# Attention: splits of the Fourier branch's projection weights ordered behind the turned probabilities three steps ahead of their use

## The chip, the core and the metric

The kernel runs on one core of one Trainium2 chip. The metric is the device time of one execution in microseconds (us), the median over runs; lower is better. Engines are named as in the profile: PE (TensorE, matmul), PEld (its weight loads), DVE (VectorE), ACT (ScalarE), POOL (GpSimd) and SP (SyncE, which issues DMAs here).

## The reference, cut to what matters

One block of a diffusion backbone, in fp32: 512 latent tokens, 256 context tokens, width 2048. Attention has 12 query heads and 4 key heads of 128; a Fourier branch of width 512 runs beside it. Both are gated, projected to width 2048 and merged.

```python
def block(qi):
    s = jnp.einsum('bqhgd,bkhd->bhgqk', qi, k, preferred_element_type=jnp.float32)
    w = jax.nn.softmax(s, axis=-1).astype(v.dtype)
    return jnp.einsum('bhgqk,bkhd->bqhgd', w, v)
...
y_a = (attn * jax.nn.silu(z_a)) @ w_pa
y_b = (_fourier_mix(u_b) * jax.nn.silu(z_b)) @ w_pb
return (g_a * y_a + g_b * y_b) @ w_o
```

The product that this case turns on is the one with `w_pb`, whose rows lie behind those of `w_pa` in one tensor, `w_pab`.

## The kernel before

**Numbers as pairs.** A fp32 operand is split into a high part (ACT, L181: a copy rounded to fp32r) and a low part (DVE, L182: the source less the high part). A product is then three matmuls (`mm3`, L339 to L341: high by high, low by high, high by low, in the order of the lines). Every weight that comes from memory is split so: it lands in a raw buffer (`wr`, L217, issued by SP; some land in one of four tiles `R`), and `split_piece` makes `whi` and `wlo` of it, 128x1024 each. The raw buffer is free for the next load once `wlo` is made.

**The attention stage.** It has 48 steps, one for each head and block of 128 queries, with a loop over `i` in the program. In a step, `scores(i)` makes 128x768 scores on PE, DVE finds their maximum (L1533), ACT takes the exponential into `probs` (L1535). `turn(i - 1)` transposes the probabilities of the step before in six 128x128 pieces on PE (L1551) into one region of PSUM, and splits them from there: ACT writes `pth` (L181, 128x768), DVE `ptl` (L182). Two turns fill one pair `pth`, `ptl` of 256 queries, and `values` multiplies a pair with the values (18 matmuls of 256 columns). The region into which probabilities are turned is one (`wide[3]`), so the next turn's transposes wait until `ptl` of the turn before has read it. Three more regions (`wide[0]` to `wide[2]`) take scores in rotation, and now and then the transposed keys of the next key head (`get_keys`, L1389). `wide[2]` and `wide[3]` share a PSUM bank.

**The filler.** Between these, `fill` puts pieces of the Fourier branch's projection on PE: for each of four chunks of 512 output columns and each of four blocks of tokens, 12 matmuls with the weights `whi`, `wlo` of two pieces of `w_pab` (in the trace: `banks<-whi,s` 128x512), into one bank; DVE multiplies it with the gate (L1499) and so frees the bank for the next block. The two pieces of the first chunk are made ahead of the attention stage. The six others bear these names in the order of the instructions: `whi_6810` and `whi_6830` (second chunk, raw `wr_6455` and `wr_6457`), `whi_7335` and `whi_7355` (third, `wr_6915` and `wr_6917`), `whi_7850` and `whi_7870` (fourth, `wr_7436` and `wr_7438`). Each `wlo` has the next number.

**Other work of the stage.** DVE also sums gate weights (L1369, 128x1024, from raw buffers), scales attention by its gate (L1577, L1587) and makes forms of the next stage's operand (L1618 to L1624). ACT scales gates by the softmax's sums (L1545) and copies turned gates out of PSUM (L1576, after the transposes L1566). `turn_queries` (L1396) turns and splits queries. POOL loads heads and gates and adds up weights for the next stage by DMA.

**What sets the order.** In the attention stage no order is written out for any engine: a scheduler places each engine's instructions by dependencies and by its own estimates of durations, working through the program in order. Once placed, ACT, DVE, POOL and SP run their queues strictly in that order, and so does PE with its matmuls. `tc.issue_after(x)` around an instruction keeps the scheduler from placing that instruction ahead of `x`; it names an order and no data. `get` (L298) splits the piece that is asked for and up to three pieces behind it in the stream (`look`), so in program order a piece of `w_pab` is split long ahead of its use. Before the change nothing held such a split back (`in_line` is empty until the last stage), and the scheduler placed it wherever ACT and DVE had room by its estimate.

Of the kernel before, what the change touches and what calls it, by code (L numbers as in the profile page):

```python
# [27 lines left out]
NKEY = T + C  # L28
KT = NKEY // P
# [44 lines left out]
def context_piece(g, name, pc):  # L74

    n = 28 * (g - NQZ) + 4 * ONE_GROUP.index(name) + pc
    if n % 2 == 0 and 0 <= n < 8:
        return "cn", n // 2
    if n % 7 == 4 and 18 <= n < 46:
        return "cr", n // 7 - 2  # L80
# [43 lines left out]
def block_kernel(ctx, tc, xT, ctx_rows, ctx_toks, x, c_row, w_ss, w_gate, vecs, qkg, rope, dft_c, dft_s,  # L124
# [32 lines left out]
    def uid(s):  # L157
        cnt[0] += 1
        return f"{s}{cnt[0]}"
# [20 lines left out]
    def split_from(src, hi, lo):  # L180
        first = nc.scalar.activation(hi, src, ACT.Copy)  # L181
        return first, nc.vector.tensor_tensor(lo, src, hi.bitcast(F32), op=ALU.subtract)  # L182
# [61 lines left out]
    def hl_tiles():  # L244
        if more_hl and not more_hl[0]:
            hl_pools.extend(range(MORE_HL))
            more_hl.clear()
        elif more_hl:
            more_hl[0] -= 1
        hl_pools.append(hl_pools.pop(0))  # L250
        pool = hl_pools[-1]
        if isinstance(pool, tuple):
            return [slot_tile(p, (1024,), F32R) for p in pool]
        if isinstance(pool, int):
            return int_tiles(pool)
        return [pool.tile([P, 1024], F32R, tag=t, bufs=hl_pools.count(pool), name=uid("w" + t)) for t in ("hi", "lo")]


    last_split, split_of, in_line, context_sub, chained = [], [], [], [], []

    look = [1]

    def split_piece(e):
        if e.out is not None or e.kind == "raw":
            return
        raws = [r for _, r in e.raws]
        src = raws.pop(0) if e.stage is None else chain[e.pc]
        for r in raws:
            nc.vector.tensor_tensor(src, src, r, op=ALU.add)
        if e.off:  # L270
            with ExitStack() as line:
                if e.key == ("P7", KV, 3):
                    line.enter_context(tc.issue_after(context_sub[-1].ins))
                if e.key[1] in DIFF_IN_LINE:

                    line.enter_context(tc.issue_after(split_of[-2][1].ins))
                nc.vector.tensor_tensor(src, chain[e.pc], src, op=ALU.subtract)
        hi, lo = e.dst() if e.dst else hl_tiles()
        if isinstance(hi, Halves):
            for k in range(2):  # L280
                last_split.append(split_from(src[:, 512 * k : 512 * k + 512].rearrange("p (a c) -> p a c", a=2),
                                             hi.parts[k], lo.parts[k]))
        else:
            hi, lo = hi[:, : e.cols], lo[:, : e.cols]
            with ExitStack() as line:
                if in_line:
                    for i in last_split[-1]:
                        line.enter_context(tc.issue_after(i.ins))
                last_split.append(split_from(src, hi, lo))
        split_of.append(last_split[-1])  # L290
        if e.nxt is not None:
            chained[:] = [nc.gpsimd.dma_start(chain[e.pc], e.nxt, accum_op=ALU.add)]  # L292
        if e.stage == 3:
            left[e.pc] = 0
        r = lambda t: t if isinstance(t, Halves) else t.rearrange("p (n m) -> p n m", n=e.n)
        e.out = (r(hi), r(lo))

    def get(key):  # L298
        load_more()
        turn = [e for e in ahead if not e.aside]  # L300
        assert turn[0].key == key, (turn[0].key, key)
        for e in turn[: min(look[0], len(hl_pools))]:
            if e is turn[0] or e.key[0] != "V":
                split_piece(e)
        load_more()
        e = turn[0]
        ahead.remove(e)
        free.extend(p[0::2] for p, _ in e.raws if p in retired)
        return e.raws[0][1] if e.kind == "raw" else e.out
# [17 lines left out]
    def take(shape, dt=F32, pool=None):  # L327
        p = next((p for p in free if p[0] is pool), free[0])
        free.remove(p)
        t = slot_tile(p, shape, dt)  # L330
        home[id(t)] = p, t
        return t

    def give(*ts):
        free.extend(home.pop(id(t))[0] for t in ts)
# [86 lines left out]
    for g in range(LAST + 1):  # L422
        for name in ONE_GROUP:
# [6 lines left out]
            for pc in range(4):  # L430
                p = context_piece(g, name, pc)
# [4 lines left out]
            for pc in range(4):  # L436
                if (g, name, pc) in GATE_AT:
                    q = GATE_AT[g, name, pc]
                    stream(("gate", q), w_gate[q], 1024, 1, "raw")
                    e = todo.pop()  # L440
# [4 lines left out]
    q = NGATE  # L445
# [300 lines left out]
    def split_next():  # L746
        e = next(e for e in ahead if e.out is None and e.kind != "raw")
        split_piece(e)
        e.raws = []
# [27 lines left out]
    with tc.manual_schedule(engines={E.PE}):  # L777
# [6 lines left out]
        with tc.manual_schedule(engines={E.Activation, E.DVE}):  # L784
# [25 lines left out]
            for kb in range(1, 4):  # L810
                k = kb + 1
# [32 lines left out]
            for kb in range(4, KK - 4, 2):  # L844
# [6 lines left out]
                k = kb + 2  # L851
# [100 lines left out]
    for g in range(4):  # L952
        gate_b(g)
        positions(g)
        if g < 2:
            tokens(g + 2)
        with behind((finals[-1], low[g if g < 2 else 3])):
            for e in ahead[:g]:
                split_piece(e)
            for z, y in products[2 * g - 4 : 2 * g - 2] if g > 1 else ():  # L960
                nc.vector.tensor_tensor(z, y, z, op=ALU.mult)
# [554 lines left out]
    probs, pts, AT, A1, A2 = {}, {}, {}, {}, {}  # L1516
# [30 lines left out]
    def turn(i):  # L1547
        p = probs.pop(i)
        tp = wide[3]
        for k in range(KT):  # L1550
            nc.tensor.transpose(tp[:, k * P : (k + 1) * P], p[:, k * P : (k + 1) * P], ident)  # L1551
        if i % 2 == 0:
            pts[i // 2] = [atp.tile([P, KT, 256], F32R, tag=n, bufs=2, name=uid(n)) for n in ("pth", "ptl")]
        c = slice((i % 2) * P, (i % 2) * P + P)
        split_from(tp[:, :NKEY].rearrange("p (k q) -> p k q", k=KT), *(w[:, :, c] for w in pts[i // 2]))
        give(p)

    def values(half):
# [127 lines left out]
    for i in range(NSTEP + 3):  # L1686
# [13 lines left out]
        if 1 <= i <= NSTEP:  # L1700
            turn(i - 1)
            divide(i - 1)
# [14 lines left out]
        if i == 3:  # L1717
            with tc.issue_after(maxima[0].ins), tc.issue_after(maxima[1].ins):
                e = take((1024,))
# [350 lines left out]
```

## Time and profile before

| what | value |
|---|---|
| median of 3 runs | 1287.12 us (1286.21 to 1287.29) |
| the profiled execution | 1286.97 us |
| its span in the profile | 1285.2 us |
| attention stage in the trace | about 803.6 to 1009 us of the span |
| granted TensorE clock, mean | 0.999 |

The profiled execution took 1286.97 us, 1.8 us more than its span. In timelines a row is start in us, duration in us, engine, line, operation, output and inputs (buffer numbers left out), shape and count; in square brackets stands how long the engine was idle before it and what ended that. Matmuls are pipelined, and the shown duration of one reaches into the next, so PE's real pace is read from the starts. An engine's row with "q" is its instruction queue.

### The profile page before, as it was taken

Reading aid. Unit: us, or ns where it says so; the run is one execution under the profiler, and the core shown is the slowest. Engines: PE = TensorE matmul, PEld = TensorE weight load, DVE = VectorE, ACT = ScalarE, POOL = GpSimd, SP = SyncE. Lnnn points to the kernel's source line nnn. Section 1 sums busy time; section 2 is a strip of 40 time slices with the busy share of each in tenths; the row PEclk is TensorE's granted clock in tenths of the full one; section 3 lists DMA queues with packets and bytes.
Section 4 is the critical chain, followed back from the end, with each engine's and each line's share of the span. In section 5 each row is a group of like instructions: output and inputs, shape, how many; then the busy total and the mean of one; then the engine's idle time right before and its main releaser. Section 6 shows DMA issues by size and latency. Waiting matters only on the chain.

```text
span 1285.2 us, 17638 instructions
## 1 busy us (share of the span) xinstructions
PE 1269.6 (99%) x6562; PEld 1045.2 (81%) x6562; DVE 991.0 (77%) x1305; ACT 683.2 (53%) x1077; POOL 173.2 (13%) x226
## 2 busy tenths in 40 slices
PE   8999999999999999999999999999999999999997
PEld 5677888888888888888888888888888888888886
DVE  5767899889778787748687756778898777787677
ACT  5322765555466564543355445766667646465544
POOL 0000121111102011012021011011100221211310
PEclk9999999999999999999999999999999999999999
DMA  9998798888898998887879897578852989998986
GB/s 378 412 368 344 242 204 254 229 240 239 234 315 209 320 271 254 291 197 188 282 204 288 254 259 234 180 234 250 265 178 67 260 241 258 245 207 222 227 207 179
DMA packets 104343, 319.07 MB, mean 248 GB/s; under 512 B 9889, under 2 KB 32801, under 8 KB 100289
## 3 DMA queue, kind: packets, MB, share of 16 engines
q1 hardware_dynamic: 54336, 195.24, 41.8%
q0 software_dynamic: 27600, 100.29, 37.0%
q10 hardware_dynamic: 22320, 22.42, 5.1%
q8 instruction: 51, 0.84, 0.3%
q14 instruction: 36, 0.29, 0.1%
HBM read 283.30 MB, written 34.61 MB: 247 GB/s over the span
## 4 chain that ended last, share of the span: by engine, by line
PE 82%; DVE 3%; DMA 2%; ACT 2%; issue 1%; SPq 0%; ACTq 0%
PE banks L339 10%; PE banks L340 10%; PE banks L341 10%; PE x L341 9%; PE x L339 9%; PE x L340 9%; PE y L341 8%; PE y L340 8%; PE y L339 8%; PE banks L1551 2%; DMA wr<-in_w_pab 1%; DVE wlo L182 1%; DMA s<-yb_d 1%; PE banks L1665 1%; DVE s L182 0%
## 5 line engine op out<-in xcount | busy, mean ns | idle before, releaser
L181 ACT ACTIVATE whi<-R 128x1024 fp32r<-128x1024 f32 x138 | 145.1, 1058 | 143.7 <-PE banks L341 47.5
L182 DVE TENSOR_TENSOR wlo<-R,whi 128x1024 fp32r<-128x1024 f32 x138 | 167.7, 1221 | 61.2 <-ACT whi L181 60.9
L182 DVE TENSOR_TENSOR wlo<-wr,whi 128x1024 fp32r<-128x1024 f32 (+1 forms) x122 | 147.3, 1213 | 62.7 <-ACT whi L181 62.5
L181 ACT ACTIVATE whi<-wr 128x1024 fp32r<-128x1024 f32 (+1 forms) x122 | 127.4, 1050 | 123.4 <-PE y L341 33.0
L339 PE MATMUL banks<-whi,s 128*128 128x512 f32 (+1 forms) x400 | 157.8, 394 | 0.9 <-ACT ev L1160 0.7
L340 PE MATMUL banks<-wlo,s 128*128 128x512 f32 (+1 forms) x400 | 155.9, 390 | 0.0
L341 PE MATMUL banks<-whi,s 128*128 128x512 f32 (+1 forms) x400 | 155.8, 389 | 0.0
L339 PE MATMUL x<-whi,s 128*128 128x512 f32 x352 | 137.1, 390 | 0.0
L341 PE MATMUL x<-whi,s 128*128 128x512 f32 x352 | 137.0, 389 | 0.0
L340 PE MATMUL x<-wlo,s 128*128 128x512 f32 x352 | 136.9, 389 | 0.0
L292 POOL DMA_DIRECT2D R<-in_w_g x68 | 59.5, 874 | 484.7 <-DVE wlo L182 290.2
L340 PE MATMUL y<-wlo,s 128*128 128x512 f32 x316 | 123.0, 389 | 0.1
L339 PE MATMUL y<-whi,s 128*128 128x512 f32 x316 | 122.9, 389 | 0.0
L341 PE MATMUL y<-whi,s 128*128 128x512 f32 x316 | 122.8, 389 | 0.0
L181 ACT ACTIVATE s<-wr 128x512 fp32r<-128x512 f32 (+2 forms) x93 | 60.8, 677 | 66.0 <-DMA wr<-cf_d 24.4
L182 DVE TENSOR_TENSOR s<-wr,s 128x512 fp32r<-128x512 f32 (+2 forms) x93 | 66.7, 749 | 31.8 <-ACT s L181 30.9
L339 PEld LDWEIGHTS banks<-whi,s 128*128 128x128 f32 x400 | 75.2, 188 | 16.6 <-ACT ev L1160 1.1
L341 PEld LDWEIGHTS banks<-whi,s 128*128 128x128 f32 x400 | 75.2, 188 | 15.3
L340 PEld LDWEIGHTS banks<-wlo,s 128*128 128x128 f32 x400 | 75.2, 188 | 13.9 <-DVE wlo L182 0.2
L340 PEld LDWEIGHTS x<-wlo,s 128*128 128x128 f32 x352 | 66.1, 188 | 13.8
L341 PEld LDWEIGHTS x<-whi,s 128*128 128x128 f32 x352 | 66.1, 188 | 13.7
L339 PEld LDWEIGHTS x<-whi,s 128*128 128x128 f32 x352 | 66.1, 188 | 13.6
(333 smaller groups left out, 2794.0 us busy)
## 6 DMA issues: line engine op xcount, KB each, us to landing
wr<-in_w_g SPq DMA_DIRECT2D x124, 512.0 KB, 5.6
R<-in_w_g POOLq DMA_DIRECT2D x68, 512.0 KB, 7.4
wa<-in_w_ss SPq DMA_DIRECT2D x31, 1024.0 KB, 9.5
R<-in_w_g SPq DMA_DIRECT2D x32, 512.0 KB, 5.8
wr<-in_w_gate SPq DMA_DIRECT2D x32, 512.0 KB, 5.1
wr<-in_w_o SPq DMA_DIRECT2D x24, 512.0 KB, 7.1
R<-in_w_o POOLq DMA_DIRECT2D x24, 512.0 KB, 8.9
wr<-in_w_pab SPq DMA_DIRECT2D x20, 512.0 KB, 6.1
```

What stands on the lines that cost most here:

```text
L181: first = nc.scalar.activation(hi, src, ACT.Copy)
L182: return first, nc.vector.tensor_tensor(lo, src, hi.bitcast(F32), op=ALU.subtract)
L292: chained[:] = [nc.gpsimd.dma_start(chain[e.pc], e.nxt, accum_op=ALU.add)]
L339: nc.tensor.matmul(o, ah, bh, start=start, stop=False, skip_group_check=cont)
L340: nc.tensor.matmul(o, ah, bl, start=False, stop=False, skip_group_check=cont)
L341: nc.tensor.matmul(o, al, bh, start=False, stop=stop, skip_group_check=cont)
L1551: nc.tensor.transpose(tp[:, k * P : (k + 1) * P], p[:, k * P : (k + 1) * P], ident)
L1665: last_turn[0] = nc.tensor.transpose(tp[:, k // 2, 256 * (k % 2) + P * t : 256 * (k % 2) + P * t + P], m[:, t, k * P : k * P + P], ident)
```

## The change

`turn` appends the two instructions of its split (`pth` on ACT, `ptl` on DVE) to a list `turned_low`. When `split_piece` splits a piece of `w_pab` for the filler (key `pab`), both of its instructions may be placed only behind the third-last pair of that list, that is, behind the split of the probabilities that were turned three turns back in program order. For the two pieces of the first chunk the list is still empty, and nothing changes. In the last stage (`in_line`) the old rule stays. No instruction is added or taken away.

```diff
-    last_split, split_of, in_line, context_sub, chained = [], [], [], [], []
+    last_split, split_of, in_line, context_sub, chained, turned_low = [], [], [], [], [], []
...
-                if in_line:
-                    for i in last_split[-1]:
-                        line.enter_context(tc.issue_after(i.ins))
+                for i in last_split[-1] if in_line else turned_low[-6:-4] if e.key[0] == "pab" else ():
+                    line.enter_context(tc.issue_after(i.ins))
                 last_split.append(split_from(src, hi, lo))
...
-        split_from(tp[:, :NKEY].rearrange("p (k q) -> p k q", k=KT), *(w[:, :, c] for w in pts[i // 2]))
+        turned_low.extend(split_from(tp[:, :NKEY].rearrange("p (k q) -> p k q", k=KT), *(w[:, :, c] for w in pts[i // 2])))
```

What the scheduler makes of it shows in the order of the instructions. The file is one line shorter from L286 on, so the rows of after bear line numbers lower by one for the same code (L1551 reads L1550 there). Up to the attention stage and after it the order is the same on every engine, except where named below.

The first place is ACT's queue where the second chunk's pieces are soon due (`pth_6718` is written twice, for two turns). Before:

```order
L181 ACTIVATE pth_6718<-banks 128x6x128
L181 ACTIVATE s_6604<-s_6601 128x256
L1545 ACTIVATE s_6263<-s_6263,gain 128x128
L1535 ACTIVATE s_6784,gain<-banks,gain 128x768
L181 ACTIVATE s_6805<-banks 128x512
L1545 ACTIVATE s_6513<-s_6513,gain 128x128
L181 ACTIVATE pth_6718<-banks 128x6x128
L181 ACTIVATE whi_7335<-wr_6915 128x1024
L1535 ACTIVATE s_6841,gain<-banks,gain 128x768
L181 ACTIVATE pth_6795<-banks 128x6x128
```

And after:

```order
L181 ACTIVATE pth_6718<-banks 128x6x128
L1575 COPY R_1342<-banks 128x256
L1544 ACTIVATE s_6513<-s_6513,gain 128x128
L181 ACTIVATE whi_6810<-wr_6455 128x1024
L181 ACTIVATE whi_6830<-wr_6457 128x1024
L181 ACTIVATE s_6604<-s_6601 128x256
L181 ACTIVATE pth_6718<-banks 128x6x128
L1534 ACTIVATE s_6784,gain<-banks,gain 128x768
L181 ACTIVATE s_6805<-banks 128x512
L181 ACTIVATE pth_6795<-banks 128x6x128
```

`whi_7335` has left the place ahead of `pth_6795` (it stands 40 rows later now, behind the first `pth_7240`), and `whi_6810` and `whi_6830` have come in ahead of the second `pth_6718`. Before, `whi_6810` stood ahead of the attention stage and `whi_6830` four rows ahead of the first `pth_6718`.

The second place is PE's queue at the same steps, between the turns of `s_6706` and `s_6735`. Before, these rows stood between the six transposes of the one and the six of the other:

```order
L341 MATMUL banks<-s_6335,s_6645 128x512
L339 MATMUL banks<-s_6335,s_6645 128x256
L340 MATMUL banks<-s_6336,s_6645 128x256
L341 MATMUL banks<-s_6335,s_6645 128x256
L339 MATMUL banks<-whi_6450,s_6409 128x512
L340 MATMUL banks<-wlo_6451,s_6409 128x512
L341 MATMUL banks<-whi_6450,s_6410 128x512
L339 MATMUL banks<-pth_6718,s_6341 128x256
L339 MATMUL banks<-s_6335,s_6645 128x512
L340 MATMUL banks<-s_6336,s_6645 128x512
L341 MATMUL banks<-s_6335,s_6645 128x512
L1551 MATMUL banks<-ident,s_6735 128x128 x6
```

And after, behind the transposes of `s_6706` and one matmul of the filler:

```order
L1395 MATMUL banks<-ident,s_6648 128x128 x4
L1388 MATMUL banks<-ident,wr_6442 128x128 x4
L338 MATMUL banks<-s_6335,s_6645 128x512
L339 MATMUL banks<-s_6336,s_6645 128x512
L340 MATMUL banks<-s_6335,s_6645 128x512
L338 MATMUL banks<-whi_6450,s_6409 128x512
L339 MATMUL banks<-wlo_6451,s_6409 128x512
L340 MATMUL banks<-whi_6450,s_6410 128x512
L338 MATMUL banks<-s_6335,s_6645 128x256
L339 MATMUL banks<-s_6336,s_6645 128x256
L340 MATMUL banks<-s_6335,s_6645 128x256
L1550 MATMUL banks<-ident,s_6735 128x128 x6
```

More of PE's work lies between the two turns now. The last two of the six transposes of keys (L1389, `wr_6442`) stand behind `s_6735`'s turn in both. Between the turn and these two came 17 matmuls of 256 columns before; now there are 3 of 512 columns and 8 of 256.

The third place is DVE's queue some twenty steps later, where the fourth chunk's first piece has come to. Before:

```order
L182 TENSOR_TENSOR ptl_7758<-banks,pth_7757 128x6x128
L1533 TENSOR_REDUCE gain<-banks 128x1
L1577 SCALAR_TENSOR_TENSOR s_7633<-banks,R_1342 128x256
L1533 TENSOR_REDUCE gain<-banks 128x1
L1544 RECIPROCAL gain<-gain 128x1
L1369 SCALAR_TENSOR_TENSOR wr_7573,gparts<-wr_7573,crow_5349 128x1024
L182 TENSOR_TENSOR ptl_7758<-banks,pth_7757 128x6x128
L182 TENSOR_TENSOR s_7867<-wr_7419,s_7866 128x768
L182 TENSOR_TENSOR s_7841<-banks,s_7841 128x512
```

And after:

```order
L182 TENSOR_TENSOR ptl_7758<-banks,pth_7757 128x6x128
L182 TENSOR_TENSOR wlo_7851<-wr_7436,whi_7850 128x1024
L1532 TENSOR_REDUCE gain<-banks 128x1
L1576 SCALAR_TENSOR_TENSOR s_7633<-banks,R_1342 128x256
L1532 TENSOR_REDUCE gain<-banks 128x1
L1543 RECIPROCAL gain<-gain 128x1
L1368 SCALAR_TENSOR_TENSOR wr_7573,gparts<-wr_7573,crow_5349 128x1024
L182 TENSOR_TENSOR s_7841<-banks,s_7841 128x512
L182 TENSOR_TENSOR ptl_7758<-banks,pth_7757 128x6x128
L182 TENSOR_TENSOR s_7867<-wr_7419,s_7866 128x768
L182 TENSOR_TENSOR wlo_7871<-wr_7438,whi_7870 128x1024
```

`wlo_7851` has come in behind the first `ptl_7758`. Before, it stood 41 rows earlier, between the two `ptl_7317`, with `whi_7850` between the two `pth_7316` on ACT.

`whi_7355` and `whi_7870` keep their places within two or three rows. On SP, the loads of the stage stand in another order (`wr_6915` behind two gate pieces and the values `wr_6894`, and a gate piece `wr_7763` five loads later), since raw buffers come free in another order. On POOL, three issues have changed places with a neighbour, and the store of the gate sums (L1746) stands five issues later.

## Prediction

> **What bounds the kernel now.** I read first the busy times of the page, then the windows of 10 us through the attention stage, and in the windows that stand out the timeline of each engine.
>
> ```profile
> PE 1269.6 (99%) x6562; PEld 1045.2 (81%) x6562; DVE 991.0 (77%) x1305; ACT 683.2 (53%) x1077; POOL 173.2 (13%) x226
> ```
>
> PE is the bound: only time in which PE waits can be won, and all that can be lost is new waiting of PE. The change touches the order of the attention stage alone (about 803.6 to 1009 us of the span of 1285.2), so I looked for PE's waits there. Windows, with busy time and instructions of PE, PEld, DVE, ACT and POOL, then the granted clock, the DMA share and GB/s:
>
> ```profile
> 830.00:840.00 10.00, 10.00 (x70) 8.89 (x69) 9.11 (x17) 7.77 (x17) 0.55 (x1) 1.00 0.84 219
> 840.00:850.00 10.00, 8.78 (x58) 7.22 (x57) 7.66 (x12) 5.97 (x10) 2.13 (x4) 1.00 0.64 217
> 890.00:900.00 10.00, 9.71 (x61) 8.12 (x60) 9.40 (x15) 6.09 (x12) 1.60 (x3) 1.00 0.74 208
> 940.00:950.00 10.00, 9.64 (x66) 8.53 (x65) 9.57 (x16) 7.22 (x14) 1.49 (x3) 1.00 0.68 209
> ```
>
> The first is a window without a wait; the three others hold PE's waits near a chunk's first weights (places A, B and C). The clock was full in all of them. PE's rows there:
>
> ```profile
> 841.26 0.39 PE L340 MATMUL banks<-s,s 128*128 128x512 f32 x1
> 841.50 0.40 PE L341 MATMUL banks<-s,s 128*128 128x512 f32 x1
> 842.30 0.87 PE L1551 MATMUL banks<-ident,s 128*128 128x128 f32 x6 [0.40 <-DVE ptl L182]
> ...
> 844.77 0.28 PE L340 MATMUL banks<-ptl,s 128*128 128x256 f32 x1
> 844.89 0.28 PE L341 MATMUL banks<-pth,s 128*128 128x256 f32 x1
> 845.99 0.44 PE L1389 MATMUL banks<-ident,wr 128*128 128x128 f32 x2 [0.82 <-DVE ptl L182]
> ...
> 891.91 0.39 PE L341 MATMUL banks<-whi,s 128*128 128x512 f32 x1
> 892.38 0.39 PE L339 MATMUL banks<-pth,s 128*128 128x256 f32 x1
> ...
> 897.26 0.39 PE L341 MATMUL banks<-s,s 128*128 128x512 f32 x1
> 897.87 0.50 PE L339 MATMUL banks<-whi,s 128*128 128x512 f32 x1 [0.22 <-DVE R L1499]
> ...
> 947.99 0.28 PE L339 MATMUL banks<-pth,s 128*128 128x256 f32 x1
> 948.62 0.39 PE L339 MATMUL banks<-s,s 128*128 128x256 f32 x1 [0.36 <-ACT s L1535]
> ```
>
> Starts tell PE's pace: a matmul of 512 columns takes 0.24 (841.26 to 841.50), one of 256 takes 0.12 (844.77 to 844.89). What is over in a step from start to start is waiting: A1, 841.50 to 842.30, 0.80 - 0.24 = 0.56; A2, 844.89 to 845.99, 1.10 - 0.12 = 0.98; B1, 891.91 to 892.38, 0.47 - 0.24 = 0.23; B2, 897.26 to 897.87, 0.61 - 0.24 = 0.37; C, 947.99 to 948.62, 0.63 - 0.12 = 0.51. Together 2.65 us, 0.2% of the time. Behind each stands a split of the filler's weights, on ACT, on DVE, or on both.
>
> **The change part by part.**
>
> Nothing is added or removed; seven of the twelve instructions for six pieces move far. One moved piece takes 0.97 us of ACT's queue (842.30 to 843.27, below) and 1.23 of DVE's.
>
> *Place A, `whi_7335` goes.* ACT's and DVE's rows:
>
> ```profile
> 836.28 0.81 ACT L181 ACTIVATE pth<-banks 128x768 fp32r<-128x768 f32 x1
> ...
> 839.83 0.81 ACT L181 ACTIVATE pth<-banks 128x768 fp32r<-128x768 f32 x1
> 842.30 1.07 ACT L181 ACTIVATE whi<-wr 128x1024 fp32r<-128x1024 f32 x1 [1.66 <-DMA wr<-in_w_pab]
> 843.27 0.88 ACT L1535 ACTIVATE s<-banks,gain 128x768 f32<-128x768 f32 x1
> ...
> 844.14 0.80 ACT L181 ACTIVATE pth<-banks 128x768 fp32r<-128x768 f32 x1
> ```
> ```profile
> 837.92 0.95 DVE L182 TENSOR_TENSOR ptl<-banks,pth 128x768 fp32r<-128x768 f32 x1
> ...
> 841.29 0.95 DVE L182 TENSOR_TENSOR ptl<-banks,pth 128x768 fp32r<-128x768 f32 x1
> ...
> 843.40 1.23 DVE L182 TENSOR_TENSOR wlo<-wr,whi 128x1024 fp32r<-128x1024 f32 x1 [0.56 <-ACT whi L181]
> 844.98 0.96 DVE L182 TENSOR_TENSOR ptl<-banks,pth 128x768 fp32r<-128x768 f32 x1 [0.35 <-ACT pth L181]
> ```
>
> ACT stood 1.66 us at `whi_7335`, whose weights had not landed. Behind it in ACT's queue stood an exponential and `pth_6795`, then on DVE `ptl_6796`, and PE's last two key transposes (L1389) waited for that: this is A2. With the split gone from here, `pth` can begin when the transposes end (842.30 + 0.87 = 843.17), 0.97 us earlier than 844.14. From their end to the next allowed transposes is 844.14 to 844.98 on ACT and 844.98 to 845.99 on DVE, 0.84 + 1.01 = 1.85 us. But PE's own order changed as well: between turn and the two L1389 stand 3 matmuls of 512 and 8 of 256 columns now, 3 x 0.24 + 8 x 0.12 = 1.68 us, counted from the start behind the transposes. Six transposes took 842.30 to 844.89 less 16 x 0.12, that is 0.67 (0.11 each), so that start lies 0.20 ahead of their modelled end. 1.85 + 0.20 - 1.68 = 0.37; with a little for ACT's start I say that 0.40 of A2's 0.98 stays and 0.58 goes.
>
> The wait is there although the two L1389 write other columns than `ptl` reads: `wide[2]` and `wide[3]` share a bank. The Trainium skill, PSUM — Partial Sum Buffer, section on bank collisions, says to guard PSUM by bank and quadrant and not by address. By that rule the 0.40 stays, and the trace agrees (0.82 us idle at 845.99, ended by `ptl`); guarded by address, it would go and the sum below would be 0.40 larger.
>
> *Place A, `whi_6810` and `whi_6830` come in.* They stand ahead of the second `pth_6718` (839.83), and the turn at 842.30 waits for that one's `ptl` (841.29): A1. From the first `pth_6718` (836.28) to the second took 3.55 us. In the new queue stand there the first itself (0.81), 2 x 0.97 of the two pieces, and a copy, a scaling and `s_6604` of at most 256 columns (0.3 each, a third of the 0.81 for 768): 3.65, 0.10 more. On DVE, from one `ptl` to the next took 3.37 (837.92 to 841.29); `wlo_6811` (1.23) has come in, while `s_6805` (512 columns, two thirds of 0.95) and idle time have left: a few tenths more at most. So I expect the second `ptl` up to 0.2 later, 0.6 if ACT's copy must wait for its transposes. PE meanwhile has more to do between the turns: 7 x 0.24 + 8 transposes of 0.11 + 3 x 0.12 = 2.92, where 7 x 0.24 + 4 x 0.12 = 2.16 stood, 0.76 more. A wait of 0.56 with 0.76 of work before it and 0.2 of delay behind it is gone; with 0.6 of delay, 0.40 of it stays. I take it as gone, 0.56. Where these two pieces stood, nothing on PE waits for them.
>
> *Place B, `whi_7850` goes and `whi_7335` comes in.*
>
> ```profile
> 884.97 0.90 ACT L1535 ACTIVATE s<-banks,gain 128x768 f32<-128x768 f32 x1 [0.58 <-DVE gain L1533]
> ...
> 895.38 1.06 ACT L181 ACTIVATE whi<-wr 128x1024 fp32r<-128x1024 f32 x1 [1.23 <-DMA wr<-in_w_pab]
> ```
> ```profile
> 887.28 0.42 DVE L1577 SCALAR_TENSOR_TENSOR s<-banks,R 128x256 f32<-128x256 f32 x1 [1.12 <-ACT R L1576]
> ...
> 888.38 0.96 DVE L182 TENSOR_TENSOR ptl<-banks,pth 128x768 fp32r<-128x768 f32 x1 [0.67 <-ACT pth L181]
> ...
> 889.63 1.23 DVE L182 TENSOR_TENSOR wlo<-wr,whi 128x1024 fp32r<-128x1024 f32 x1
> ...
> 891.64 0.68 DVE L182 TENSOR_TENSOR s<-banks,s 128x512 fp32r<-128x512 f32 x1
> ...
> 896.73 0.42 DVE L1577 SCALAR_TENSOR_TENSOR s<-banks,R 128x256 f32<-128x256 f32 x1 [0.59 <-ACT R L1576]
> 897.14 0.67 DVE L1499 TENSOR_TENSOR R<-banks,R 128x512 f32<-128x512 f32 x1
> ```
>
> B2: ACT stood 1.23 us for the weights of `whi_7850`; behind it the copy of turned gates (L1576), DVE's L1577 and L1499 ran late, and L1499 frees the bank that the filler waited for (897.87). The piece is gone from here, and 0.37 with it. B1: PE waits for the split at 891.64, which stands behind `wlo_7356` (889.63). In the new order `wlo_7356` stands behind that split and a gate: 0.23 goes. `whi_7335` comes in just ahead of the exponential at 884.97, where ACT has 0.58 of idle time; `wlo_7336` comes where DVE has 1.12 + 0.67 of it, more than its 1.23. I cost it at nothing; without that cover it costs up to 1.23. Its DMA will have landed (see the loads below).
>
> *Place C, `whi_7850` comes in at about 933 us.*
>
> ```profile
> 947.59 0.90 ACT L1535 ACTIVATE s<-banks,gain 128x768 f32<-128x768 f32 x1
> ```
> ```profile
> 934.77 0.96 DVE L1533 TENSOR_REDUCE gain<-banks 128x1 f32<-128x768 f32 x1 [0.71 <-PE banks L341]
> ...
> 936.59 0.96 DVE L1533 TENSOR_REDUCE gain<-banks 128x1 f32<-128x768 f32 x1 [0.54 <-PE banks L341]
> ```
>
> `wlo_7851` adds 1.23 on DVE; DVE's idle time ahead of the next two reductions is 0.71 + 0.54 = 1.25. It fits with 0.02 to spare, so I expect no cost, but this is the weakest cover. The wait at 948.62 is for the exponential at 947.59. In the new order 5 of the filler's matmuls (5 x 0.24 = 1.2) stand ahead of the scores that wait, more than the 0.51; of it I take 0.40, leaving something for the narrow cover.
>
> *Loads.* SP's loads of the stage and three of POOL's issues change order, since raw buffers are held longer. The loads of this kind land 6.1 us after issue:
>
> ```profile
> wr<-in_w_pab SPq DMA_DIRECT2D x20, 512.0 KB, 6.1
> ```
>
> Followed through the raw buffers, each is issued over 15 us ahead of its use in either order (an estimate from the places of the issues); no cost, and one late load would cost up to 6.1.
>
> *The sum:* 0.58 + 0.56 + 0.37 + 0.23 + 0.40 = 2.14 us. Does it pass through? Behind the stage PE hardly waits for anything that time would not bring along:
>
> ```profile
> PE banks L1665 <- DMA s<-yb_d: 0.7, 1, 0.7
> ```
>
> This is PE's one wait after 1009 us that a DMA ends, and its 0.7 us may stay. So the profiled 1286.97 us (1.8 above its span, 0.15 below the median) would become 1284.8, and the median 1287.12 becomes 1284.98.
>
> **The rivals.**
>
> *1. More goes than the five waits.* Weight loads stop as well when PE is held back by less than a whole matmul. PEld falls from 8.89 in the quiet window to 7.22, 8.12 and 8.53: 1.67 + 0.77 + 0.36 = 2.80, and at 0.889 a us that is 3.15 us of PE's time near the three places. If all goes, 1287.12 - 3.15 = 1284.0. For it: ACT's queue loses both long DMA waits (1.66 and 1.23). Against it: A2's 0.40 should stay. Perfetto Trace Analysis in the Trainium skill (Identifying the Most-Contended Engine) has it that matmul busy time is a poor measure for TensorE and weight-load busy time a good one. By matmul busy time the three windows miss only 1.22 + 0.29 + 0.36 = 1.87 us, which would give 1285.25; the five waits by starts are 2.65, so the trace agrees that busy time shows too little.
>
> *2. Given back at C.* If DVE's gaps at 934 no longer come where they did, one piece's 1.23 ends on PE's path and C's 0.40 isn't won: 1284.98 + 0.40 + 1.23 = 1286.6. For it: 0.02 of margin.
>
> *3. Slower.* DVE is the second engine, 9.40 and 9.57 of 10 us at B and C. If `whi_7850`, `wlo_7851` and then `whi_7870`, `wlo_7871` end last on the chain from scores to turned probabilities, each piece costs 1.06 on ACT and 1.23 on DVE in a row: 2 x 2.29 = 4.58, and C's 0.40 is lost: 1284.98 + 4.98 = 1290.0. It decides once PE's reductions at 934 to 937 leave less than the 1.23 us that move in. Against it: filler work on PE covers a late turn for about 1 us each.
>
> *4. The waits are replaced by others.* The scheduler's order rests on its estimates of durations; the same pieces go through the same engines, and PE may wait as long elsewhere: 1287.1.
>
> **How the numbers follow.** My forecast, the sum, has a chance of 0.42 and a range of its own of 1284.3 to 1285.7 (A2's 0.40 also gone and 0.3 elsewhere; A1's 0.40 and 0.3 of C staying). Rival 1 has 0.24, rival 2 0.14, rival 3 0.10, rival 4 0.10. About 0.2% of 1287, 2.6 us, is what a measurement of this kernel can tell from no change: below 1284.55 is faster, above 1289.7 slower. A third of the forecast's own range, 0.14, lies below, and rival 1: 0.38 faster. The rest of the forecast, 0.28, and rivals 2 and 4 make 0.52 same. Rival 3 makes 0.10 slower. The range goes from rival 1 with another 0.6 (the quiet window itself may hold small waits) to rival 4 with 0.3: 1283.4 to 1287.4; rival 3 lies outside.
>
> **What would show each step.** In the profile after: ACT's idle time ended by DMA of `in_w_pab` in the stage should fall from 1.66 + 1.23 to nearly nothing (A2, B2). The turn that stood at 842.30 should follow its predecessor without a wait, and the two key transposes wait some 0.4. At 933 DVE should run `wlo_7851` without a later row on PE waiting for a reduction, an exponential or a turn. PEld near the three places should come to about 8.5 of 10 us each. The prediction is wrong if PE waits over 0.5 us anywhere that it didn't (first at C, then ahead of 884.97), or if a load ends ACT's idle time at a new place.

## The result, and the profile after

| kernel | median of runs, us | lowest to highest | runs |
|---|---|---|---|
| before | 1286.71 | 1286.21 to 1287.29 | 6 |
| after | 1293.62 | 1292.93 to 1294.03 | 6 |

The ratio is 1.0053, with a 95% interval of 1.004 to 1.0066: 6.9 us slower, where 2.1 us faster was forecast. The profiled execution of after took 1293.67 us, its span is 1291.9 (1285.2 before). The first line of the page says that PE did the same matmuls with 1.9 us more of busy time, and so stood idle about 5 us longer:

```profile
PE 1271.5 (98%) x6562; PEld 1047.7 (81%) x6562; DVE 990.7 (77%) x1305; ACT 682.0 (53%) x1077; POOL 174.4 (13%) x226
```

**In this pair of profiles the attention stage won about what was forecast.** The four windows of the prediction, now in after (columns as there):

```profile
830.00:840.00 10.00, 10.00 (x69) 9.07 (x68) 8.73 (x16) 8.10 (x15) 0.55 (x1) 1.00 0.74 208
840.00:850.00 10.00, 9.95 (x65) 8.26 (x64) 9.52 (x16) 5.93 (x13) 2.75 (x5) 1.00 0.80 269
890.00:900.00 10.00, 10.00 (x70) 9.09 (x69) 9.35 (x14) 5.81 (x12) 2.42 (x4) 1.00 0.80 270
940.00:950.00 10.00, 10.00 (x71) 8.99 (x70) 9.40 (x15) 7.25 (x14) 1.59 (x4) 1.00 0.69 261
```

PE is busy all through at B and C, and for all but 0.05 us at A. The view of PE's waits in the stage keeps one line, at its start; before there were five:

```profile
PE banks L338 <- ACT ev L1159: 0.7, 1, 0.7
```

PE came to the stage 0.18 us earlier than before (its first matmul of the filler starts at 803.42, before at 803.60) and left it 2.00 us earlier. The loss lies behind the stage. These are the last matmul ahead of the first transposes of a merged chunk (L1665 before, L1664 after), the transposes, and one matmul some way on, in before and then in after:

```profile
1033.37 0.40 PE L341 MATMUL banks<-whi,s 128*128 128x512 f32 x1
1033.61 1.04 PE L1665 MATMUL banks<-ident,s 128*128 128x128 f32 x8
...
1036.99 0.39 PE L341 MATMUL banks<-whi,s 128*128 128x512 f32 x1
```
```profile
1031.37 0.39 PE L340 MATMUL banks<-whi,s 128*128 128x512 f32 x1
1036.03 1.97 PE L1664 MATMUL banks<-ident,s 128*128 128x128 f32 x8 [4.27 <-DMA s<-yb_d]
...
1042.18 0.40 PE L340 MATMUL banks<-whi,s 128*128 128x512 f32 x1
```

The same matmul starts 2.00 us earlier at 1031.37 and 5.19 later at 1042.18: 7.19 us went in 11. Of these, 4.42 are the wait for a chunk of `yb_d` that is summed by DMA, and 2.77 are lost in the next 6 us although PE is busy: the eight transposes take 1.97 and not 1.04. The windows of after show why, in the third number from the end, the granted clock:

```profile
1030.00:1036.00 6.00, 1.76 (x8) 1.13 (x6) 1.23 (x1) 1.06 (x1) 0.54 (x1) 0.91 1.06 268
1036.00:1042.00 6.00, 5.97 (x19) 5.06 (x20) 1.40 (x2) 3.02 (x3) 0.96 (x2) 0.52 1.06 254
1084.00:1090.00 6.00, 6.00 (x30) 4.98 (x29) 5.32 (x5) 4.04 (x5) 1.72 (x2) 1.00 1.06 205
```

The clock fell to half during the wait and stayed there until 1041.8. Behind a second wait for `yb_d`, 0.90 us at 1083.35, it stayed full. That second wait and small ones behind it bring the difference to 6.57 us at the last matmul (1283.96 against 1277.39).

**Why the chunk came late.** POOL issues that sum (L1651 before, L1650 after). POOL's rows of before and of after:

```profile
989.01 1.20 POOL L1746 DMA_DIRECT2D gs<-gcol  x1 [14.92 <-DVE gcol L1745]
...
1019.01 0.87 POOL L1651 DMA_DIRECT2D s<-yb_d  x1 [0.71 <-DVE s L1649]
```
```profile
1002.51 1.19 POOL L1745 DMA_DIRECT2D gs<-gcol  x1 [0.46 <-issue]
...
1017.00 0.87 POOL L1650 DMA_DIRECT2D s<-yb_d  x1 [0.72 <-DVE s L1648]
```

The sum itself is issued on time, 2.0 us earlier. What has moved is the store of the gate sums, `gs<-gcol`, from 30.0 us to 14.5 us ahead of the sum's issue. The DMA view of 985 to 1045 us, with KB each and us from issue to landing, before and then after:

```profile
s<-g_d POOLq DMA_DIRECT2D x6, 512.0 KB, 9.4
...
s<-yb_d POOLq DMA_DIRECT2D x1, 512.0 KB, 9.6
gs<-gcol POOLq DMA_DIRECT2D x1, 8.0 KB, 11.2
```
```profile
s<-g_d POOLq DMA_DIRECT2D x6, 512.0 KB, 13.1
...
s<-yb_d POOLq DMA_DIRECT2D x1, 512.0 KB, 19.0
gs<-gcol POOLq DMA_DIRECT2D x1, 8.0 KB, 14.5
```

In before the store of 8 KB takes longer to land than a load of 512 KB. It writes a column of 128 partitions by 16 into rows, 2048 pieces of 4 bytes. Before, the sum landed at 1019.01 + 9.6 = 1028.6, 5.0 us ahead of its use at 1033.61; after, at 1017.00 + 19.0 = 1036.0, which is PE's start. The windows around the store, before and after:

```profile
989.00:1001.00 12.00, 12.00 (x77) 10.38 (x76) 11.61 (x17) 10.56 (x20) 4.07 (x5) 1.00 0.44 17
```
```profile
1002.00:1014.00 12.00, 12.00 (x64) 10.31 (x63) 9.86 (x15) 8.40 (x13) 3.49 (x6) 1.00 0.51 83
...
1006.00:1015.00 9.00, 9.00 (x46) 7.64 (x45) 7.83 (x11) 5.53 (x8) 2.50 (x4) 1.00 0.41 26
...
1018.00:1042.00 24.00, 19.73 (x80) 16.14 (x79) 7.53 (x7) 9.23 (x9) 3.76 (x5) 0.86 1.05 295
```

While the store is under way little moves (17 GB/s in 12 us of before; 26 in 9 us of after, where transfers issued ahead of the store still ran to about 1006), and then a backlog runs at full share. Before, that blank lay at 989 to 1001. Its first 3 us would have been empty anyway, since nothing else was issued between 984 and 991.9, and the backlog was gone in time. Now it lies 13 us later, where the next stage's loads and the sum are issued.

The store moved since the second of two tiny sums on DVE ahead of it moved. DVE's rows, before and then after:

```profile
988.18 0.15 DVE L1744 TENSOR_TENSOR gcol<-gparts 128x16 f32<-128x16 f32 x1
988.37 0.18 DVE L1745 TENSOR_TENSOR gcol<-gcol,small 128x16 f32<-128x16 f32 x1
```
```profile
986.97 0.16 DVE L1743 TENSOR_TENSOR gcol<-gparts 128x16 f32<-128x16 f32 x1
...
1001.70 0.17 DVE L1744 TENSOR_TENSOR gcol<-gcol,small 128x16 f32<-128x16 f32 x1
```

The scheduler, with other instructions free at other times, put 21 others between the two.

### The profile page after: what moved, and what is told of

Its sections match the earlier page's. It is cut to its first block, busy times and chain, and to the rows that moved or that the text cites. A ratio compares the mean times of both kernels' runs of the same rounds, so it can differ in the third digit from the quotient of the medians.

```text
span 1291.9 us, 17642 instructions
## 1 busy us (share of the span) xinstructions
PE 1271.5 (98%) x6562; PEld 1047.7 (81%) x6562; DVE 990.7 (77%) x1305; ACT 682.0 (53%) x1077; POOL 174.4 (13%) x226
## 4 chain that ended last, share of the span: by engine, by line
PE 89%; DMA 5%; issue 2%; DVE 2%; ACT 1%; POOL 1%; SPq 0%; POOLq 0%; ACTq 0%; DVEq 0%
PE x L340 9%; PE x L338 9%; PE x L339 9%; PE banks L338 9%; PE banks L340 8%; PE banks L339 8%; PE y L339 8%; PE y L340 8%; PE y L338 8%; DMA s<-yb_d 3%; PE banks L1550 2%; PE pd L566 2%; PE pc L338 1%; PE pb L338 1%; PE pc L340 1%
```

## The experiments

The theory, S: the late store of 4-byte pieces holds up DMA and so makes the summed chunk late; PE waits and then runs at half clock; the splits' new order itself is a gain. The rival, L: the other order of the weight loads, with raw buffers held longer, makes the chunk late. Every ratio is against runs of before on the same chip (median 1286.24 to 1286.59 us).

### 1. Before, with the store late

```diff
-    nc.vector.tensor_tensor(gcol, gcol, bada[:, 2 * KK :], op=ALU.add)
+    with tc.issue_after(turned_low[-1].ins):
+        nc.vector.tensor_tensor(gcol, gcol, bada[:, 2 * KK :], op=ALU.add)
```

(`turn` fills `turned_low` as in after; no split looks at it.)

> The kernel before, with only the store of the gate sums moved on POOL's queue to the place that it has after the change (behind the second load of the first gates); nothing of the splits' order is changed. Theory S (the store of 2048 pieces of 4 bytes holds POOL's DMA queue for some 12 us, and at the late place this pushes the summed chunk of yb_d past the transposes that need it): PE stands about 4.3 us at those transposes, then some 8 us run at a lower clock for 2.9 us more, and 1.3 us of small waits follow: 1286.7 + 8.5 = 1295, at least 1292. Theory L (the other order of the weight loads on SP and the raw buffers held longer make the chunk late, and the store's place is incidental): 1286.7.

Measured: 1295.58 us (1293.19 to 1296.99), ratio 1.007 (1.0057 to 1.0082). POOL's row, the chunk's DMA and PE's wait:

```profile
1008.37 1.19 POOL L1747 DMA_DIRECT2D gs<-gcol  x1 [4.03 <-DVE gcol L1746]
```
```profile
s<-yb_d POOLq DMA_DIRECT2D x1, 512.0 KB, 21.7
```
```profile
1040.83 1.97 PE L1665 MATMUL banks<-ident,s 128*128 128x128 f32 x8 [7.03 <-DMA s<-yb_d]
```

With every split where it was (only the second tiny sum and the store have changed place), the kernel before becomes slower than after. The store alone does it, and L falls as the main cause. The store came out 4 us later than in after (on the clock of before), and the wait is 2.8 us longer.

### 2. After, with the store early

```diff
             if n == 2 * KK - 1:
+                nc.vector.tensor_tensor(gparts[:, :KK], gparts[:, :KK], bada[:, 2 * KK :], op=ALU.add)
...
-    nc.vector.tensor_tensor(gcol, gcol, bada[:, 2 * KK :], op=ALU.add)
```

> The kernel after, with the bias added to the first half of the gate sums ahead of the last sum, so that one sum is left and the store goes out at the place on POOL's queue that it had before the change. The splits' order stays that of after. Theory S: the loss behind the attention stage goes and the 2.0 us won in it stay: 1286.7 - 2.0 = 1284.7, the summed chunk of yb_d lands some 10 us after its issue. Theory L: 1293.6, with the chunk landing 19 us after its issue.

Measured: 1285.63 us (1284.44 to 1285.99), ratio 0.9991 (0.9982 to 1.0). The order of all engines is that of after, but for the store and the moved sum. POOL's row, the chunk, and PE's waits for it behind the stage:

```profile
988.21 1.19 POOL L1745 DMA_DIRECT2D gs<-gcol  x1 [16.76 <-DVE gcol L1744]
```
```profile
s<-yb_d POOLq DMA_DIRECT2D x1, 512.0 KB, 11.0
```
```profile
PE banks L1664 <- DMA s<-yb_d: 0.9, 2, 0.5
```

The 4.27 us and the half clock are gone: 8 us between the medians of after and of this kernel, for the place of one store. S holds from both sides. The gain that is left, 0.8 us by the medians, is smaller than the 2.0 expected; where the rest went is told below.

### 3. After, with the store in rows

```diff
+    grow = const.tile([KK, P], F32, name="grow")
...
-    nc.gpsimd.dma_start(gs.rearrange("k p -> p k"), gcol)
+    nc.tensor.transpose(b1()[:KK, :P], gcol, ident)
+    nc.scalar.copy(grow, b1()[:KK, :P])
+    nc.gpsimd.dma_start(gs, grow)
```

> The kernel after, with the gate sums turned by one small transpose on PE and stored as 16 rows of 512 bytes instead of 2048 pieces of 4 bytes, at a late place on POOL's queue (one issue later than in after). Theory S as a matter of the pieces: the store lands within some 3 us and holds nothing up, 1284.7 to 1285.2. If it is the late place of any store that matters, not its pieces: about 1293. Theory L: 1293.6.

Measured: 1285.89 us (1285.16 to 1287.26), ratio 0.9998 (0.9989 to 1.0006). The store stands two issues later than in after, not one. Issued at 1009.24, the same 8 KB land in 5.3 us (not within 3), and the chunk in 10.4:

```profile
s<-yb_d POOLq DMA_DIRECT2D x1, 512.0 KB, 10.4
gs<-grow POOLq DMA_DIRECT2D x1, 8.0 KB, 5.3
```

So it isn't a late store as such that makes the loss, but its 2048 pieces. PE still waits 1.3 us for the chunks of `yb_d` here, and the time is 0.7 us above the expected range. The Trainium skill, DMA: Bandwidth & Descriptors, says under "Why small descriptors are slow" that each piece has a fixed overhead, and in its "Specifications" that a transfer needs 512 bytes for line rate. The pair of 14.5 and 5.3 us for 8 KB agrees, and tells the size of it here.

### 4. The store early, only the third and fourth chunk held back

```diff
-                for i in last_split[-1] if in_line else turned_low[-6:-4] if e.key[0] == "pab" else ():
+                for i in last_split[-1] if in_line else turned_low[-6:-4] if e.key[0] == "pab" and CHUNKS.index(e.key[1]) in (2, 3) else ():
```

(With the second experiment's two lines as well, as in 6, 7 and 8.)

> As the kernel after with the store early, but only the pieces of the third and fourth chunk are held back; those of the second stand as before the change. By the prediction's terms A2, B1, B2 and C belong to the third and fourth chunk and the place A1 partly to the second. With the second chunk's pieces away, A1 and A2 are both served by the missing whi_7335: 1286.7 - (0.56 + 0.98 + 0.23 + 0.37 + 0.4) = 1284.2 if the second chunk's pieces only cost; 1285.3 if the gain at A came from PE's own new order, which goes with them. If all 2.0 us came from elsewhere: 1286.7.

Measured: 1285.26 us (1284.66 to 1286.82), ratio 0.9992 (0.9984 to 1.0001). That is the second expectation's number, but it isn't told apart from the second experiment, and the interval reaches from near the first expectation almost to the third. It decides nothing between them.

### 5. After, the store issued by SP

```diff
-    nc.gpsimd.dma_start(gs.rearrange("k p -> p k"), gcol)
+    nc.sync.dma_start(gs.rearrange("k p -> p k"), gcol)
```

> The kernel after, its store of the gate sums issued by SP and not by POOL, still as 2048 pieces of 4 bytes and at about the same time (1002 us). If the store holds up what is queued behind it in POOL's own DMA queue, the gates' loads and the summed chunk of yb_d pass it now: the chunk lands some 10 us after issue and the time is 1284.7 to 1286; SP's loads of weights behind the store may come late instead. If the pieces load the 16 DMA engines whoever issues them, the chunk is late as in after: about 1293.

Measured: 1289.98 us (1288.27 to 1291.64), ratio 1.0029 (1.0018 to 1.004). SP's row, the chunk's DMA and PE's wait:

```profile
1001.90 0.37 SPq L1745 DMA_DIRECT2D gs<-gcol  x1
```
```profile
s<-yb_d POOLq DMA_DIRECT2D x1, 512.0 KB, 18.0
```
```profile
1035.01 1.97 PE L1664 MATMUL banks<-ident,s 128*128 128x128 f32 x8 [3.27 <-DMA s<-yb_d]
```

The time lies between the two expectations. In the profile the other queue spares 1.0 us of the 4.27, and the chunk still lands 18.0 us after its issue, against 19.0 in after and 9 to 11 in the runs without a late store of pieces. So the pieces also stand in the way of transfers on other queues: a load of 512 KB that SP issues at about 1005 lands after 13.0 us in after, with the store on POOL's queue, and after 3.5 us in the third experiment (here, behind the store on SP's own queue, after 11.9). The time is another matter: by the ratios some 3.1 of the 6.9 us are spared, more than this profile shows (it is of one of the slower executions). How much of the loss hangs on POOL's own queue stays open. The pieces themselves can be seen here: from 985 to 1045 us 2433 packets are under 512 bytes, in after 417.

### 6. The store early, only the second chunk held back

The diff is that of the fourth with `in (1,)`.

> As the kernel after with the store early, but only the second chunk's two pieces are held back, those of the third and fourth stand as before. By the prediction's terms B1, B2 and C are not won, and at place A whi_7335 still waits for its weights, though PE has more work between the turns: 0.56 of A1 at most, so 1286.4 - 0.6 = 1285.8. If the gain at A comes mainly from PE's new order there, 1.1 (A1 and A2): 1285.3. Not slower than before in any theory.

Measured: 1286.05 us (1285.12 to 1289.16), ratio 0.9999 (0.9991 to 1.0008): nearer to the first expectation, and no gain that can be measured. But in its profile PE took as little time for the stage as in after; what was won was lost at the transposes of two chunks of `yb_d`:

```profile
PE banks L1664 <- ACT whi L181: 1.1, 1, 1.1
PE banks L1664 <- DMA s<-yb_d: 1.0, 1, 1.0
```

So the prices of the places don't add up by chunk: in 4 and in 6 the stage takes about 1.8 us less in the profile, with other pieces held back, and what the medians show of it hangs on waits behind the stage. (How much of the 1.8 us is owed to one profile of before is told below.)

### 7 and 8. The store early, the pieces held one turn less, and two turns more

`turned_low[-8:-6]` and `turned_low[-2:]` in place of `turned_low[-6:-4]`.

> As the kernel after with the store early, with the pieces held behind the fourth-last turn and not the third-last, so each may stand one step earlier. If what counts is that a piece's weights have landed when ACT comes to it, one step (4 us) less of delay still leaves that, and the time is that of the kernel after with the store early, 1285.6, within 0.5. If the exact place among ACT's and DVE's gaps counts, it may lose up to 1 us of the gain: 1286.4.

> As the kernel after with the store early, with the pieces held behind the last turn and not the third-last, so that both pieces of a chunk stand together, close to their use. If the delay is harmless as long as PE has other work, 1285.6 again. If the filler's matmuls now wait for the second split (1.06 on ACT and 1.22 on DVE for each piece, two pieces in a row, three times), PE loses 1 to 2 us at each chunk: 1287 to 1291.

Measured: 1287.39 us (1286.38 to 1288.7), ratio 1.0009 (1.0 to 1.0017), and 1290.07 us (1289.31 to 1291.99), ratio 1.0031 (1.002 to 1.0042). The largest waits of PE in the stage, of the seventh and then the eighth:

```profile
PE banks L338 <- ACT pth L181: 0.9, 1, 0.9
```
```profile
PE banks L1550 <- ACT s L1534: 2.0, 2, 1.3
PE banks L338 <- ACT pth L181: 0.9, 1, 0.9
```

The seventh misses both of its expectations. The eighth's time lies in its second range, but by luck: none of these waits is a filler matmul's for a split. They are for exponentials and turns, at 947 (1.34 us, in the eighth) and at the stage's end (992 to 998). At the stage's end all pieces had long been split. At 947 that isn't so: the fourth chunk's two `wlo` ran on DVE in a row from 942.45 to 944.8, with the reduction for the late exponential right behind them, so there they may have a share, which isn't shown. The other order of the pieces brings another order of what follows. The distance of three turns isn't a safe optimum: one turn less loses all that is won.

In the eighth the clock fell as well, inside the stage:

```profile
998.00:1001.00 3.00, 3.00 (x10) 2.53 (x11) 2.42 (x4) 1.74 (x4) 0.28 (x1) 0.50 0.69 26
```

It fell at about 997.7, behind waits of 0.65, 0.90 and 0.50 us with three matmuls among them, and cost some 1.6 us (3.15 us from 997.87 to 1001.02 for ten matmuls that take 1.57 at full clock). In the seventh waits of 0.90 and 0.50 us at the same place left it full.

### 9. Before, with the store in the middle

The diff is that of the first with `turned_low[-3]`.

> The kernel before, with the store of the gate sums one place earlier on POOL's queue than in the first experiment (behind the first load of the gates and the next weights, ahead of the second load), at about 1001 us. By the theory of the store the wait for the summed chunk of yb_d grows with the store's time: none at 989, 4.3 us at 1002.5 in after (1004.5 on the clock of before, which is 2.0 us later there), 7.0 us at 1008.4. Worked out on that line, 2 to 3 us of waiting here, and with the slow clock behind it 1289 to 1292. If a slow clock needs a longer wait than this, 1288.5 to 1289.5. If it is the place behind the second gate load that decides and not the time: 1286.4.

Measured: 1293.23 us (1292.2 to 1294.47), ratio 1.0053 (1.0039 to 1.0067).

```profile
1003.48 1.21 POOL L1747 DMA_DIRECT2D gs<-gcol  x1 [4.49 <-DVE gcol L1746]
```
```profile
1037.29 1.57 PE L1665 MATMUL banks<-ident,s 128*128 128x128 f32 x8 [3.77 <-DMA s<-yb_d]
```

The store came at 1003.5, not 1001, and the time lies above the expected range. The wait of 3.8 stands on the line: none for 989.0, 3.8 for 1003.5, 4.3 for 1004.5 (after, on the clock of before), 7.0 for 1008.4. From 1003.5 on the wait grows by 0.5 to 0.7 us for each us of the store.

### 10. Before, with the store in rows

The diff is that of the third, on before.

> The kernel before with the gate sums turned on PE and stored as 16 rows of 512 bytes, late on POOL's queue. It tells whether the 2048 small pieces cost the kernel before anything at their early place: if they do, by the waits for yb_d behind the stage (0.7 us in its profile), 1285.7; if not, 1286.4. Nothing slower than 1287, else a late store of any form costs.

Measured: 1287.3 us (1286.76 to 1288.08), ratio 1.0006 (0.9997 to 1.0015). The median lies 0.3 us above the 1287 that the expectation allowed, and the interval reaches from a little faster to 0.15% slower. So no gain shows from taking the pieces away: at 989 us they cost the kernel before nothing that was measured, though the load issued behind them (991.95 in before) lands after 12.7 us there and after 6.0 here. It had that to spare. Whether a late store in rows costs a little stays open: PE's wait for `yb_d` behind the stage is 1.6 us here, 1.3 in the third experiment and 0.7 in before.

## Why the prediction was wrong, point by point

**What bounds: right. The attention stage: right in kind, in size partly by luck.** To compare stretches with another order of matmuls, I took PE's starts, gave each matmul its pace (0.228 us for 512 columns, 0.1175 for 256, 0.109 for a transpose) and summed what is over, by stretches of the span. In us:

| stretch | 833-862 (A) | 862-884 | 884-908 (B) | 908-931 | 931-955 (C) | 955-1008 |
|---|---|---|---|---|---|---|
| before | 2.68 | 0.99 | 1.45 | 0.76 | 1.39 | 1.49 |
| after | 1.56 | 1.16 | 0.65 | 1.07 | 0.98 | 1.58 |
| gain | 1.12 | -0.17 | 0.80 | -0.31 | 0.41 | -0.09 |
| forecast | 1.14 | | 0.60 | | 0.40 | |

The three places sum to 2.33 where 2.14 was forecast; 0.6 was given back between them, so 1.8 us were won in the stage. The DMA waits of `whi_7335` and `whi_7850` on ACT are gone. One term was off: of A2's wait, 0.40 was to stay. PE's rows in after, and the weight load's:

```profile
843.19 0.28 PE L339 MATMUL banks<-ptl,s 128*128 128x256 f32 x1
843.51 0.44 PE L1388 MATMUL banks<-ident,wr 128*128 128x128 f32 x2
```
```profile
843.51 0.20 PEld L1388 LDWEIGHTS banks<-ident,wr 128*128 128x128 f32 x2 [0.25 <-DVE ptl L182]
```

The 0.32 us between the starts are a matmul of 0.12 and a wait of 0.20, ended by `ptl` as the prediction had it, at half the size. So A2 won 0.78 and not 0.58, and some 0.2 was lost again in small waits around it, which brings A to the 1.12. At C the narrow cover of 0.02 us held; rivals 2 and 3, which rested on it, did not happen.

**A2 was not in every execution.** Four profiles have the old order at A. PE stood 0.82 us at the two key transposes in the one that the prediction used, 0.48 in experiment 9, and no wait shows there in 1 and 10. In 10 the split that was late came at 841.10 after 0.58 us of waiting, not at 842.30 after 1.66:

```profile
841.10 1.06 ACT L181 ACTIVATE whi<-wr 128x1024 fp32r<-128x1024 f32 x1 [0.58 <-DMA wr<-in_w_pab]
```

By the same sums A was 2.68, 2.35, 1.75 and 1.75 us in these four (before, 9, 1, 10), and the whole stage 8.8, 8.1, 7.6 and 7.8, where after, 2 and 3 have 6.9 to 7.0. The wait for a load is a matter of that load's landing, and one profile had an unlucky one. So the stage won 1.8 us against the profile that the prediction was made from, and 0.6 to 1.1 against the three others; that the three places together came close to the forecast is partly luck. This is one reason why the medians show a smaller gain than the forecast. Another, smaller, is that in experiment 2 PE waited 0.9 us for chunks of `yb_d` behind the stage, where the profile of before shows 0.7.

**Loads and POOL's issues: this step failed.** The prediction put the change of order on SP and POOL at "no cost", and asked of each only whether it would land ahead of its own use. The store of gate sums moved five issues, and what it writes is not read before 1097.5 us, so by that question it was free. What it costs is what it does to the others: some 9 us (1006 to 1015) in which the DMA engines move next to nothing else, and the backlog behind them. Its price stood in the trace of before, as 11.2 us for 8 KB and a blank of 17 GB/s at 989 to 1001, and wasn't looked up. The loads on SP, which I followed with care, were not the cause (experiment 2 keeps their order).

**"Does it pass through": failed with it.** I took PE's one DMA wait behind the stage, 0.7 us, for all that could stay. The right reading was the slack of the transfers that had no wait. The chunk that became late had 5.0 us, and nothing in a list of waits shows that.

**The clock: not in the prediction.** 2.77 of the 6.9 us are half clock. The Trainium skill, TensorE: Matmul & The Clock Gate, section "What's actually happening", has it that an idle window of about 3.4 us halves the clock and about as much busy time restores it. The runs agree only in part. The clock fell with single waits of 3.27, 3.77, 4.27 and 7.03 us (experiments 5 and 9, after, experiment 1) and stayed full with one of 1.6 us (experiment 10). But in experiment 5 it was down some 2.4 us into the wait, and in experiment 8 it fell with no wait over 1.34 us in the whole stage, behind three short ones close together. So the length of one wait doesn't tell. The half clock lasted 6.8 us in after and 3.4 in experiment 9, and the slow stretch behind the wait cost 1.7 to 2.8 us, by the comparison shown for after, with no more behind the longest. (The 3.27 us count from a modelled end; from the last matmul's start and its pace they are 3.43.) Each of the four waits of over 3 us thus cost 1.7 to 2.8 us more than itself.

**The rivals.** The forecast of slower stood on a mechanism at C that did not occur; the loss came from a mechanism that no rival named.

**What stays open.** Why the scheduler put 21 others between the first gate sum and the second wasn't tried; that it hangs on which instructions its estimates find ready is an inference. By what means the pieces hold up transfers on other queues isn't shown. Whether the kernel with the store early is truly faster than before is at the edge of what was measured: ratios of 0.9991 and 0.9992, with intervals that reach 1.0 and 1.0001.

## What to carry to other kernels

When a change sets a scheduler free, read the whole difference of the order, and for each moved DMA ask what it holds up, not only whether it arrives in time itself: the number to look up is its time to landing against its bytes. Look for slack, not for waits, behind the place of the change; a transfer with 5.0 us to spare became late here when it landed 9.4 us later after its issue than before. A small store in pieces of 4 bytes belongs where little else moves, or is to be turned into rows first.

## What the hardware showed

8 KB in 2048 pieces took 10.7 to 15.9 us to land, and 5.3 and 5.8 as 16 rows of 512 bytes. While the pieces were under way, loads on another queue came late as well: with the store on POOL's queue a 512 KB load that SP issued at about 1005 us took 13.0 us (after), and 3.5 with the store in rows (experiment 3); with the store on SP's queue POOL's chunk took 18.0 us (experiment 5). TensorE's granted clock fell to 0.50 in a wait of 3.27 us and stayed there for some 5.8 us of matmuls (experiment 5); in experiment 8 it fell to 0.50 behind three waits of 0.5 to 0.9 us within 3.3 us (994.62 to 997.87).
